# Two MLPs on one core: VectorE and ScalarE in a written order, weights three products ahead, own tiles for the second pair

## The chip, the cores and the metric

The kernel runs on one core of one Trainium2 chip. The metric is the device time of one execution in microseconds (us); the median of three runs of the kernel before is 1119.15 us (1118.34 to 1121.95).

A core has a matrix engine (TensorE, PE in the profile, with its weight loads as PEld), three engines for elementwise work (VectorE = DVE, ScalarE = ACT, GpSimd = POOL), and a SyncE (SP) that here only issues transfers. Each engine works through its own list of instructions in order and waits on semaphores for the others. Matmuls write to PSUM, which is eight banks of 128 x 512 float32; everything else lies in SBUF.

## The reference, cut to what matters

Two layers on x (512 tokens, 1024 features, float32). Layer 0 mixes with stick-breaking attention, layer 1 with a gated linear recurrence; the change touches neither. Both end in the same MLP:

```python
D_MODEL, SEQ, DEPTH, D_FF = 1024, 512, 2, 4096

def squared_relu_mlp(h, w1, w2):          # w1: 1024 x 4096, w2: 4096 x 1024
    u = jax.nn.relu(h @ w1)
    return (u * u) @ w2

def reference(x, ...):
    for layer in range(DEPTH):
        h = rms_norm(x, norm_mix[layer])
        x = x + (stick_breaking_attention(h, ...) if layer % 2 == 0 else rglru_block(h, ...))
        h = rms_norm(x, norm_mlp[layer])
        x = x + squared_relu_mlp(h, mlp_w1[layer], mlp_w2[layer])
    return rms_norm(x, norm_final)
```

## The kernel before, in words

**Operands in two parts.** Every matrix operand is split into a high part of type fp32r, copied by ScalarE (`wh`, `xgh`, `bh`, `sh`), and a low part, the rest, subtracted by VectorE (`wl`, `xgl`, `bl`, `sl`). Each product of two blocks is then three matmuls (high x high, high x low, low x high). So every weight block costs a ScalarE copy of 128 x 1024 (line 1002), a VectorE subtraction of the same size (line 1003), and a place in the pool `wpool`, which holds four pairs `wh`, `wl`.

**The MLP in quarters.** The 4096 hidden features are worked off in four quarters of 1024 (`q4`). A quarter has an up part (h @ w1 for its 1024 columns, in two pairs p of 512) and a down part (times its 1024 rows of w2, in two groups g of 512 rows, added into the output tiles `c`). Quarter 0's up part is eight plain slabs (`squared`, line 790 on); the up parts of quarters 1 to 3 (`up`, line 898 on) and all down parts (`down`, line 1057 on) use a scheme of seven block products, P1 to P7, in place of eight. For this, weight blocks are added into each other: b11 is used for P1, then b12 is added for P5, then b22 for P6, then b21 for P4; b12 becomes P7's operand when b22 is added. These additions are done by VectorE (line 1022) for P5 and P6, and for P7 and P4 by a transfer from DRAM that adds into the tile (line 1017, issued by POOL). An up part is 2 x 7 products of 24 matmuls with 256 columns; a down part is 2 x 7 products of 12 matmuls with 512 columns. So a quarter has 28 products.

**From up to down.** The four results of a pair lie in one tile `u` of four slots (two halves i each). Products that share a PSUM bank are taken apart by copies into `kept` (line 926) and one VectorE instruction each (line 939). Relu and square follow on ScalarE (lines 940 and 788). The down part of a group needs seven operand blocks of its pair: the slots 0 to 2 as they are (split by lines 825 and 826 into blocks 0 to 2) and four sums of slots (line 835) as blocks 3 to 6. Group 0's blocks lie in `bh`, `bl`, group 1's in `sh`, `sl`. P1 needs block 0, P2 block 1, P5 block 5, P6 block 3, P3 block 4, P7 block 6, P4 block 2. There is one buffer for `u`, so pair 1's `u` is written when pair 0's has been split.

**What sets the order.** PE keeps the order of the program text: the down part is P1 0, P5 0, P1 1, P2 0, P5 1, and so on (name and group). For ScalarE, VectorE, POOL and SP a scheduler chooses the order at build time from its own timeline, with hints in the text (`tc.high_priority()`, `tc.issue_after(...)`). A product's weights are prepared in the text right before its matmuls (in the last quarter two to three products ahead). SP loads the weight blocks into six `b` tiles and the b21 blocks into three `raw` tiles. After each product of group 1, two collects add its banks into `c` (line 1046 on VectorE; line 1049 on ScalarE for the first use in layer 0). In quarter 0's down part of each MLP, VectorE and ScalarE also form the sums of x that the later up parts need (`sums_of_x`, `halves_of_sums`, lines 853 to 891).

Of the kernel before, what the change touches and what calls it, by code (L numbers as in the profile page):

```python
# [17 lines left out]
P = 128  # L18
# [30 lines left out]
def hybrid_encoder(  # L49
# [678 lines left out]

    class Mlp:
# [51 lines left out]
        def u_tile(self, p):  # L781

            if p not in self.u:
                self.u[p] = self.mp.tile([P, 2, 4, HS], F32, tag="u", name="u", bufs=1)
            return self.u[p]

        def square(self, t):
            self.squares = A.activation(t, t, AF.Square)

        def squared(self, c):  # L790
# [11 lines left out]
            A.activation(t, ps.rearrange("p (h n) -> p h n", h=2), AF.Relu)  # L802
# [19 lines left out]
        def split(self, p, i, of, to):  # L822
            h, l = (t[:, i, to, :] for t in self.places(p))
            u = self.u[p][:, i, of, :]
            self.high = A.copy(h, u)  # L825
            self.ready = V.tensor_tensor(l, u, f(h), ALU.subtract)  # L826

        def sums(self, p, i):

            u = self.u[p]  # L830
            for out, x, y, op in (
                (2, 3, 2, ALU.subtract), (3, 0, 3, ALU.subtract), (0, 2, 0, ALU.subtract),
                (1, 0, 1, ALU.add),
            ):
                V.tensor_tensor(u[:, i, out, :], u[:, i, x, :], u[:, i, y, :], op)
# [17 lines left out]
        def sums_of_x(self, k):  # L853
# [3 lines left out]
            for c in (k, C // 2 + k):  # L857
                g = col(f"mlp{self.layer}")[:, c : c + 1]
                with tc.issue_after(self.high.ins):
                    A.activation(x[c], x[c], AF.Identity, scale=g)  # L860
            with tc.issue_after(self.ready.ins):
                V.tensor_tensor(v[:, hi], u[:, hi], v[:, hi], ALU.subtract)
            V.tensor_tensor(u[:, hi], u[:, lo], u[:, hi], ALU.subtract)
            V.tensor_tensor(u[:, lo], v[:, hi], u[:, lo], ALU.subtract)
            V.tensor_tensor(v[:, lo], u[:, lo], v[:, lo], ALU.add)
# [12 lines left out]
        def halves_of_sums(self, k):  # L878
# [6 lines left out]
            A.copy(self.s2(k), u[:, lo])  # L885
            V.tensor_tensor(low[:, lo], u[:, lo], f(self.s2(k)), ALU.subtract)
            A.copy(s3, u[:, hi])
            V.tensor_tensor(low[:, hi], u[:, hi], f(s3), ALU.subtract)
            low = self.low(C // 2 + k)
            A.copy(self.s41[:, k, :], v)  # L890
            V.tensor_tensor(low, v, f(self.s41[:, k, :]), ALU.subtract)

        def replace(self):

            for i, t in enumerate(self.s3):
                A.copy(xgh[:, 2 * i : 2 * i + 2, HS:], f(t).rearrange("p (k n) -> p k n", k=2))

        def up(self, q4, p, unit, far):

            u = self.u_tile(p)  # L900
            banks, kept = {}, {}
            for name in ("P1", "P5", "P6", "P3", "P7", "P2", "P4"):
                w = [t.rearrange("p j n -> p (j n)") for t in self.block(unit, name, far)]
                w = [t.rearrange("p (k n) -> p k n", n=2 * P) for t in w]
                block, _, _, to, *_ = self.PRODUCTS[name]
                new = to not in banks
                if new:
                    banks[to] = self.bank()
                ps = banks[to]
                for i in range(2):  # L910
                    for k in range(C // 2):
                        h, l = self.xa(block, k)
                        wh, wl = (t[:, k, i * P : (i + 1) * P] for t in w)
                        for n, (m, y) in enumerate(((wh, h), (wl, h), (wh, l))):
                            PE.matmul(  # L915
                                ps[:, i * HS : (i + 1) * HS], m, y,
                                start=new and i == k == n == 0,
                                stop=i == 1 and k == C // 2 - 1 and n == 2,
                                skip_group_check=not new,
                            )  # L920
                three = ps.rearrange("p (i n) -> p i n", i=2)
                if name in ("P1", "P5", "P6", "P7"):

                    tag = "sq" if name in ("P1", "P7") else "r"
                    t = work.tile([P, S], F32, tag=tag, name="kept")
                    A.copy(t, ps)
                    kept[name] = t.rearrange("p (i n) -> p i n", i=2)
                if name in ("P1", "P5", "P6"):
                    continue
                slot, x, y, op = {  # L930
                    "P3": (1, three, kept.get("P6"), ALU.subtract),
                    "P7": (2, kept.get("P5"), kept.get("P7"), ALU.subtract),
                    "P2": (0, kept.get("P1"), three, ALU.add),
                    "P4": (3, three, None, None),
                }[name]
                t = u[:, :, slot, :]
# [607 lines left out]
```

## Time and profile before

| | |
|---|---|
| median of 3 runs | 1119.15 us |
| profiled execution, its own time | 1119.22 us |
| its span (first to last instruction) | 1117.5 us |
| granted TensorE clock, mean | 0.978 |
| MLP of layer 0 | about 250 to 600 us of the span |
| MLP of layer 1 | about 757 us to the end |
| first product of a down part, layer 0 | 294.17, 376.74, 464.20, 550.66 us |
| first product of a down part, layer 1 | 801.74, 885.53, 974.09, 1062.67 us |
| first product of an up part, layer 0 | 335.03, 424.74, 511.20 us |
| first product of an up part, layer 1 | 845.17, 933.82, 1022.43 us |

The starts are read from the timeline of PE (first matmul of each product). Windows between such starts show how long a stretch of known products took, how long each engine was busy in it, and which clock TensorE was granted (1.00 is full speed). A stretch that takes longer than the same products elsewhere has waits or a low clock in it.

### The profile page before, as it was taken

How to read it: one execution, taken by the hardware profiler on the slowest of the kernel's cores; microseconds unless marked ns; L12 is line 12 of the kernel's file. 1: busy time of each engine (PE TensorE's matmuls, PEld its weight loads, DVE VectorE, ACT ScalarE, POOL GpSimd, SP SyncE). 2: the span in 40 equal slices, each digit the busy share in tenths (PEclk: the TensorE clock that was granted, in tenths of full speed). 3: DMA queues.
4: the chain of work that ended last, by engine and by line, in shares of the span. 5: the costliest groups of instructions: out<-in, count | busy, mean ns of one | idle time of the engine just before them, and what ended most of it. 6: DMA issues, size and time to landing. Idle time of an engine off the chain costs nothing.

```text
span 1117.5 us, 15833 instructions
## 1 busy us (share of the span) xinstructions
PE 1059.0 (95%) x5868; PEld 910.4 (81%) x5868; DVE 865.9 (77%) x1118; ACT 680.5 (61%) x1037; POOL 201.1 (18%) x242
## 2 busy tenths in 40 slices
PE   9999999999999989989989999999989989979987
PEld 7888898888779779869868777888879869958965
DVE  7778787756796977977888778854797876976886
ACT  6767676645676635735745587746574834743754
POOL 2444443400101000000002563000000000000012
PEclk9999999999999989999989999999999989989989
DMA  7746454446456655655732784242356655555533
GB/s 234 195 118 164 112 148 100 151 136 250 75 161 138 151 163 133 152 151 144 206 60 91 184 193 132 79 167 80 65 147 153 147 134 152 142 131 154 152 54 94
DMA packets 53693, 156.27 MB, mean 140 GB/s; under 512 B 8816, under 2 KB 9584, under 8 KB 53616
## 3 DMA queue, kind: packets, MB, share of 16 engines
q1 hardware_dynamic: 43536, 120.13, 33.8%
q0 software_dynamic: 9504, 34.61, 19.2%
q8 instruction: 46, 0.75, 0.3%
q10 hardware_dynamic: 576, 0.52, 0.1%
q14 instruction: 31, 0.25, 0.1%
HBM read 133.22 MB, written 4.19 MB: 123 GB/s over the span
## 4 chain that ended last, share of the span: by engine, by line
PE 63%; DVE 15%; ACT 10%; issue 7%; DMA 4%; POOL 1%; SPq 0%; ACTq 0%; POOLq 0%; DVEq 0%
PE ps_t L1035 8%; PE ps_acc L1035 6%; PE ps_z L915 6%; PE ps_acc L212 4%; PE ps_acc L210 4%; PE ps_acc L211 4%; PE ps_o L915 4%; DVE wl L1003 3%; PE ps_acc L915 3%; DMA b<-in_w_up 3%; ACT wh L1002 2%; DVE c L1046 2%; DVE sl L826 2%; PE ps_o L210 2%; PE ps_o L211 2%
## 5 line engine op out<-in xcount | busy, mean ns | idle before, releaser
L1002 ACT CAST wh<-b 128x1024 fp32r<-128x1024 f32 x168 | 174.0, 1047 | 176.9 <-DVE b L1022 79.4
L1003 DVE TENSOR_TENSOR wl<-b,wh 128x1024 fp32r<-128x1024 f32 x168 | 204.8, 1225 | 75.7 <-ACT wh L1002 75.5
L198 ACT CAST wh<-raw 128x512 fp32r<-128x512 f32 (+2 forms) x88 | 69.4, 818 | 47.1 <-DMA raw<-in_w_in 10.2
L1017 POOL DMA_DIRECT2D b<-in_w_dn x32 | 28.1, 877 | 364.9 <-DVE b L1022 238.9
L210 PE MATMUL ps_acc<-xgh,wh 128*128 128x512 f32 x208 | 85.0, 408 | 1.0 <-ACT wh L179 1.0
L205 DVE TENSOR_TENSOR wl<-raw,wh 128x512 fp32r<-128x512 f32 (+2 forms) x78 | 71.3, 941 | 18.3 <-ACT wh L198 18.1
L211 PE MATMUL ps_acc<-xgh,wl 128*128 128x512 f32 x208 | 81.6, 392 | 0.3 <-DVE wl L180 0.3
L212 PE MATMUL ps_acc<-xgl,wh 128*128 128x512 f32 x208 | 81.5, 392 | 0.1
L1017 POOL DMA_DIRECT2D b<-in_w_up x24 | 20.9, 871 | 305.6 <-DVE b L1022 198.4
L562 DVE TENSOR_TENSOR_SCAN scan<-keep,later 128x128 f32<-128x128 f32 (+1 forms) x64 | 58.0, 909 | 18.0 <-ACT keep L552 9.5
L1022 DVE TENSOR_TENSOR b<-b,b 128x1024 f32<-128x1024 f32 x56 | 68.3, 1219 | 0.4
L566 POOL TENSOR_TENSOR w<-w,scan 128x128 f32<-128x128 f32 (+1 forms) x64 | 51.9, 813 | 55.7 <-DVE scan L562 52.9
L1035 PE MATMUL ps_acc<-wh,sh 128*128 128x512 f32 x64 | 31.8, 496 | 26.5 <-ACT sh L825 18.2
L1035 PE MATMUL ps_t<-wh,sl 128*128 128x512 f32 x126 | 50.1, 397 | 5.7 <-DVE sl L826 5.7
L915 PE MATMUL ps_z<-xgh,wh 128*128 128x256 f32 x192 | 54.2, 282 | 0.0
L915 PE MATMUL ps_z<-xgh,wl 128*128 128x256 f32 x192 | 54.2, 282 | 0.0
L1035 PE MATMUL ps_t<-wh,sh 128*128 128x512 f32 x126 | 50.1, 398 | 4.0 <-ACT sh L825 4.0
L915 PE MATMUL ps_acc<-low,wh 128*128 128x256 f32 x192 | 53.7, 280 | 0.0
L1035 PE MATMUL ps_t<-wl,sh 128*128 128x512 f32 x126 | 49.8, 395 | 0.2 <-DVE wl L1003 0.2
L1035 PE MATMUL ps_t<-wh,bh 128*128 128x512 f32 x126 | 49.6, 394 | 0.0
L1035 PE MATMUL ps_t<-wl,bh 128*128 128x512 f32 x126 | 49.2, 391 | 0.0
L1035 PE MATMUL ps_t<-wh,bl 128*128 128x512 f32 x126 | 49.2, 390 | 0.0
(405 smaller groups left out, 3455.4 us busy)
## 6 DMA issues: line engine op xcount, KB each, us to landing
b<-in_w_dn SPq DMA_DIRECT2D x48, 512.0 KB, 5.9
b<-in_w_up SPq DMA_DIRECT2D x36, 512.0 KB, 3.5
b<-in_w_dn POOLq DMA_DIRECT2D x32, 512.0 KB, 5.5
b<-in_w_up POOLq DMA_DIRECT2D x24, 512.0 KB, 5.6
raw<-in_w_m SPq DMA_DIRECT2D x16, 512.0 KB, 3.9
raw<-in_w_dn SPq DMA_DIRECT2D x16, 512.0 KB, 4.5
raw<-in_w_in SPq DMA_DIRECT2D x16, 512.0 KB, 4.7
raw<-in_w_qk SPq DMA_DIRECT2D x12, 512.0 KB, 3.7
```

The source lines that it names most:

```text
L198: A.copy(wh[:, k, :], raw[:, k, :])
L205: V.tensor_tensor(wl[:, k, :], raw[:, k, :], f(wh[:, k, :]), ALU.subtract)
L210: PE.matmul(ps, wh, ah, start=start, stop=False)
L211: PE.matmul(ps, wl, ah, start=False, stop=False)
L212: PE.matmul(ps, wh, al, start=False, stop=stop)
L562: V.tensor_tensor_scan(sc[:, S - n : S][:, ::-1], keep[:, :n][:, ::-1], later[:, S - n :][:, ::-1], 1.0, ALU.mult, ALU.max,)
L566: G.tensor_tensor(wt, wt, sc[:, S - n + 1 : S + 1], ALU.mult)
L915: PE.matmul(ps[:, i * HS : (i + 1) * HS], m, y, start=new and i == k == n == 0, stop=i == 1 and k == C // 2 - 1 and n == 2, skip_group_che ...
L1002: A.copy(wh, raw)
L1003: self.cut = V.tensor_tensor(wl, raw, f(wh), ALU.subtract)
L1022: self.sum = V.tensor_tensor(raw, raw, unit[to], ALU.add)
L1035: PE.matmul(ps, m, y[:, jj, cols], start=first and n == 0, stop=last and n == 2, skip_group_check=not new,)
```

## The change

What it does:

- A wrapper `Ordered` around VectorE and ScalarE chains each instruction that the MLP issues through it behind the one before, so these two engines keep the order of the text. (In the profile all such instructions then carry one line, that of the wrapper.) The ScalarE collects of layer 0 and the plain slabs are not wrapped.
- One loop `run` over all products of the four quarters replaces `up`, `down` and the loop over quarters. Entering step i, `leave(i - 1)` first issues what follows the product that has just been queued on PE, and with it `prepare(i + 3)`: the weights of the product three further on. An up part's P7 weights are made together with P2's.
- Pair 1's four results lie in four work tiles (two `sq`, two `r`), which also take the copies that were in `kept`. Each slot is split into its operand block when its product is done (block 1 after P3, block 2 after P7, block 0 after P2); of the four sums block 5 is split first, blocks 3, 4 and 6 between the first down products (`waiting`). Pair 0's blocks 3 to 6 are split during pair 1's first products.
- The transfers that add for P7 and P4 are issued right after the weights of P5 and P6 have been cut. In every down part P6's addition for group 0 becomes such a transfer as well. That is eight more transfers of 512 KB in the program and eight fewer VectorE additions.
- Half of the sums of x (k = 0, 1) moves from quarter 0's down part into its slabs, and the squares of x stand with the first two slabs instead of the second to fifth. Quarter 0's down order becomes "mid" (P1 1 ahead of P2 0); the last one of layer 1 has P2 1 behind P5 1.

The diff, cut:

```diff
+    class Ordered:
+        def __getattr__(self, name):
+            def do(*args, **kwargs):
+                with tc.issue_after(self.prev.ins) if self.prev else nullcontext():
+                    ins = getattr(self.e, name)(*args, **kwargs)
+                if self.on:
+                    self.prev = ins
+                return ins
...
         def __init__(self, ctx, layer):
+            self.V, self.A = Ordered(V), Ordered(A)
...
-            self.high = A.copy(h, u)
-            self.ready = V.tensor_tensor(l, u, f(h), ALU.subtract)
+            self.A.copy(h, u)
+            self.ready = self.V.tensor_tensor(l, u, f(h), ALU.subtract)
...
+        def slots_of(self, p):
+            if p == 0:
+                u = self.u_tile(p)
+                return [u[:, :, j, :] for j in range(4)]
+            tags = ("sq", "sq", "r", "r")
+            return [
+                work.tile([P, S], F32, tag=t, name="u").rearrange("p (i n) -> p i n", i=2) for t in tags
+            ]
+        def split_slot(self, p, t, to):
+            h, l = (a[:, :, to, :] for a in self.places(p))
+            self.A.copy(h, t)
+            self.V.tensor_tensor(l, t, f(h), ALU.subtract)
...
         ORDERS = {
-            "first": "P1 0 P5 0 P2 0 P1 1 P5 1 P6 0 P6 1 P3 0 P3 1 P7 0 P7 1 P2 1 P4 0 P4 1",
             "mid": "P1 0 P5 0 P1 1 P2 0 P5 1 P6 0 P6 1 P3 0 P3 1 P7 0 P7 1 P2 1 P4 0 P4 1",
-            "last": "P1 0 P5 0 P2 0 P1 1 P2 1 P5 1 P6 0 P6 1 P3 0 P3 1 P7 0 P7 1 P4 0 P4 1",
+            "last": "P1 0 P5 0 P1 1 P2 0 P5 1 P2 1 P6 0 P6 1 P3 0 P3 1 P7 0 P7 1 P4 0 P4 1",
         }
+        UP = "P1", "P5", "P6", "P3", "P7", "P2", "P4"
...
+            FARS = [("P6", 0)]
+            def make(i):
...
+                name = steps[i][3]
+                ws[i] = made[i] = self.operand(self.source(unit(i), name))
+                for before, x in (("P5", "P7"), ("P6", "P4")):
+                    if name == before:
+                        self.added(unit(i), x)
+            def prepare(i):
+                if i < len(steps) and steps[i][0] == "up" and steps[i][3] == "P7":
+                    return
+                if i - 1 in range(len(steps)) and i - 1 not in made and i > 2:
+                    make(i - 1)
+                if i < len(steps) and steps[i][0] == "down":
+                    add(i, 0)
+                    if waiting and place(i) in (20, 22, 23):
+                        self.split_slot(*waiting.pop(0))
+                make(i)
+                for n in range(i + 1, i + 6):
+                    add(n, n - i)
...
+            def leave(i):
+                ahead = i + 4
...
+                if kind == "down":
+                    if p:
+                        for n in range(2):
+                            self.collect(name, n, bank[n])
+                    prepare(ahead)
...
+                if op:
+                    self.V.tensor_tensor(u[at], x, y, op)
+                if name == "P4":
+                    self.A.activation(u[3], three, AF.Relu)
+                    self.square(u[3])
+                    if p:
+                        last_sums(u, self.SUMS[:2])
...
+                prepare(ahead)
...
+                elif name == "P4" and p:
+                    last_sums(u, self.SUMS[2:3])
+                    self.split_slot(p, u[2], 5)
+                    last_sums(u, self.SUMS[3:])
+                    waiting[:] = [(p, u[j], 3 + j) for j in (0, 1, 3)]
...
+            for i, (kind, q4, g, name) in enumerate(steps):
+                load(i)
+                leave(i - 1)
```

How instructions move, at two places on VectorE. First, quarter 2 of layer 0 after pair 1's blocks 0 to 2: `u` is pair 1's results, `sl` the low parts of its blocks, `wl` a weight's low part, `b11<-b11,b12` an addition for P5, `b11<-b11,b22` one for P6, `c` a collect. Before:

```order
L1003 TENSOR_TENSOR wl_5154<-b11_4832,wh_5153 128x1024
L835 TENSOR_TENSOR u_4834<-u_4834 128x2x256
L1003 TENSOR_TENSOR wl_5173<-b11_4828,wh_5172 128x1024
L1046 SCALAR_TENSOR_TENSOR c0_3126<-ps_t_5081,rr_3442,c0_3126 128x512
L1022 TENSOR_TENSOR b11_4832<-b11_4832,b22_5075 128x1024
L835 TENSOR_TENSOR u_4834<-u_4834 128x2x256
L1046 SCALAR_TENSOR_TENSOR c0_3126<-ps_t_5082,rr_3442,c0_3126 128x512
L835 TENSOR_TENSOR u_4834<-u_4834 128x2x256
L1003 TENSOR_TENSOR wl_5190<-b11_4832,wh_5189 128x1024
L835 TENSOR_TENSOR u_4834<-u_4834 128x2x256
L1003 TENSOR_TENSOR wl_5208<-b22_5073,wh_5207 128x1024
L826 TENSOR_TENSOR sl_5029<-u_4834,sh_5028 128x1024 x2
```

The same place now, from the first of the four sums:

```order
L738 TENSOR_TENSOR u_4850<-u_4851,u_4850 128x512
L738 TENSOR_TENSOR u_4851<-u_4848,u_4851 128x512
L738 TENSOR_TENSOR wl_5091<-raw_5088,wh_5090 128x1024
L738 TENSOR_TENSOR u_4848<-u_4850,u_4848 128x512
L738 TENSOR_TENSOR sl_5012<-u_4850,sh_5011 128x2x256
L738 TENSOR_TENSOR u_4849<-u_4848,u_4849 128x512
L738 TENSOR_TENSOR wl_5113<-b11_4735,wh_5112 128x1024
L738 TENSOR_TENSOR wl_5132<-b11_4731,wh_5131 128x1024
L738 SCALAR_TENSOR_TENSOR c0_3126<-ps_t_5098,rr_3470,c0_3126 128x512
```

The four sums stood among four weights' low parts, two collects and an addition, and all of blocks 3 to 6 were split behind them; now one weight stands among the sums, and block 5 is split ahead of the last sum and of P5 1's weights (`wl_5113`).

Second, where pair 1's slots are written. Before, behind both splits of pair 0's blocks 3 to 6 (`bl`):

```order
L826 TENSOR_TENSOR bl_82<-u_4593,bh_81 128x1024
L1022 TENSOR_TENSOR b11_4828<-b11_4828,b12_4830 128x1024
L826 TENSOR_TENSOR bl_82<-u_4593,bh_81 128x1024
L1003 TENSOR_TENSOR wl_5097<-b11_4828,wh_5096 128x1024
L939 TENSOR_TENSOR u_4834<-ps_o_4871,kept_4927 128x2x256
L939 TENSOR_TENSOR u_4834<-kept_4896,kept_4989 128x2x256
L939 TENSOR_TENSOR u_4834<-kept_4864,ps_o_5000 128x2x256
```

Now, from the last split of pair 0:

```order
L738 TENSOR_TENSOR bl_82<-u_4615,bh_81 128x1024
L738 TENSOR_TENSOR u_4849<-ps_o_4878,u_4849 128x512
L738 TENSOR_TENSOR wl_4979<-b11_4731,wh_4978 128x1024
L738 TENSOR_TENSOR b11_4731<-b11_4731,b12_4733 128x1024
L738 TENSOR_TENSOR u_4850<-u_4850,u_4851 128x512
L738 TENSOR_TENSOR sl_5012<-u_4849,sh_5011 128x2x256
L738 TENSOR_TENSOR wl_5016<-b11_4731,wh_5015 128x1024
L738 TENSOR_TENSOR sl_5012<-u_4850,sh_5011 128x2x256
L738 TENSOR_TENSOR u_4848<-u_4848,ps_o_5025 128x512
L738 TENSOR_TENSOR wl_5052<-b11_4735,wh_5051 128x1024
L738 TENSOR_TENSOR b11_4735<-b11_4735,b12_4971 128x1024
L738 TENSOR_TENSOR sl_5012<-u_4848,sh_5011 128x2x256
```

The three instructions that write slots stood in one run; now each stands at its own product, with the split of its block close behind, and a weight for the coming down part at each.

More of the change, by code (lines that the diff above doesn't have):

```diff
@@ L889, in halves_of_sums @@
             low = self.low(C // 2 + k)
[L890 to L891 removed]
+            self.A.copy(self.s41[:, k, :], v)
+            self.V.tensor_tensor(low, v, f(self.s41[:, k, :]), ALU.subtract)
         def replace(self):
             for i, t in enumerate(self.s3):
[L896 to L936, printed above, removed]
[L937 to L947 removed]
@@ L1100, in hybrid_encoder, with order, part @@
-        FAR_UP, FAR_DOWN = ('P7', 'P4'), ('P7', 'P4')
-        def quarters(self, between, far, end):
-            for c in range(C):
+        def order(self, kind):
+            order = self.ORDERS[kind].split()
+            return [(name, int(g)) for name, g in zip(order[::2], order[1::2])]
+        def part(self, sums, name, g, w):
+            to = self.PRODUCTS[name][3]
+            if to not in sums:
+                sums[to] = [self.bank() for _ in range(2)]
+            for i in range(2):
+                self.times(name, g, i, w, sums[to][i], name in ("P1", "P5", "P2"))
@@ L1104, in quarters @@
+        def quarters(self, between, end):
+            for c in range(C - 1):
                 self.squared(c)
@@ L1192, in hybrid_encoder @@
         end.ready = back
-        mlp.quarters(between, ("P7", "P4"), end)
+        mlp.quarters(between, end)
         begin = [bank("acc") for _ in range(2)]
@@ L1473, in hybrid_encoder @@
         end.ready = factors
-        mlp.quarters(between, ("P7", "P4"), end)
+        mlp.quarters(between, end)
 COLS = {}
```

295 lines of the change are left out of this document (186 added, 109 removed).

## The prediction

> **What bounds the kernel now.** I read the page first, then PE's waits, then windows of equal work.
>
> ```profile
> PE 1059.0 (95%) x5868; PEld 910.4 (81%) x5868; DVE 865.9 (77%) x1118; ACT 680.5 (61%) x1037; POOL 201.1 (18%) x242
> PEclk9999999999999989999989999999999989989989
> PE ps_acc L1035 <- ACT sh L825: 18.2, 6, 4.1
> PE ps_acc L1035 <- ACT wh L1002: 8.3, 2, 4.4
> PE ps_t L1035 <- DVE sl L826: 5.7, 6, 1.1
> ...
> PE ps_z L915 <- ACT kept L926: 1.1, 2, 0.8
> ...
> PE ps_acc L915 <- ACT kept L926: 0.5, 1, 0.5
> ```
>
> PE is the bound, and what it loses it loses in few places: the longest waits (total us, times, longest) are all at line 1035, the down products, and most are for `sh`, `sl`, pair 1's operands. The clock dips at the same spots. Windows tell what these spots cost. Columns: length, then busy us (and count) of PE, PEld, DVE, ACT, POOL, granted clock, DMA share, GB/s. The first six run from the first product of each down part of quarters 1 to 3, in both layers, to the product behind P5 1: five products, six in the last.
>
> ```profile
> 376.74:400.00 23.26, 17.33 (x63) 12.61 (x62) 19.18 (x20) 12.12 (x15) 2.61 (x3) 0.86 0.63 126
> 464.20:486.58 22.38, 16.17 (x63) 11.79 (x62) 19.20 (x20) 12.02 (x15) 2.63 (x3) 0.92 0.65 131
> 550.66:574.18 23.52, 17.29 (x62) 12.76 (x61) 18.13 (x19) 12.12 (x15) 1.75 (x2) 0.86 0.41 80
> 885.53:908.86 23.33, 17.31 (x62) 12.62 (x61) 19.29 (x20) 12.12 (x15) 2.60 (x3) 0.85 0.63 125
> 974.09:997.35 23.26, 17.36 (x63) 12.61 (x61) 19.19 (x20) 12.13 (x15) 2.62 (x3) 0.86 0.61 125
> 1062.67:1087.09 24.42, 19.20 (x75) 14.65 (x73) 19.83 (x21) 12.97 (x16) 1.73 (x2) 0.86 0.25 38
> sum 140.17, PE 104.66 PEld 77.03 DVE 114.82 ACT 73.48 POOL 13.95; mean PE 17.44 PEld 12.84 DVE 19.14 ACT 12.25 POOL 2.32
> ...
> 486.58:511.20 24.62, 24.62 (x109) 20.27 (x108) 18.15 (x20) 8.39 (x8) 0.86 (x1) 1.00 0.49 139
> 511.20:550.66 39.46, 39.46 (x337) 39.46 (x336) 31.37 (x32) 28.00 (x35) 3.49 (x4) 1.00 0.71 198
> ```
>
> The last two rows are the undisturbed measure: nine down products in 24.62 us, so 2.74 each, and an up part of 14 products in 39.46. The six windows hold 31 products, 31 x 24.62/9 = 84.8 us at that pace. They took 140.17. **55.4 us** are lost there, some in waits, the rest at half clock behind them.
>
> Why PE waits there is in VectorE's and ScalarE's timeline of the second one (start, us, engine, line; in brackets idle time and its releaser). P4 of pair 1 ends at 464.2.
>
> ```profile
> 462.73 0.68 DVE L939 TENSOR_TENSOR u<-ps_o,kept 128x512 f32<-128x512 f32 x1
> ...
> 470.61 1.76 DVE L826 TENSOR_TENSOR sl<-u,sh 128x1536 fp32r<-128x1536 f32 x1 [1.46 <-ACT sh L825]
> 472.28 1.22 DVE L1003 TENSOR_TENSOR wl<-b,wh 128x1024 fp32r<-128x1024 f32 x1
> 473.42 0.68 DVE L835 TENSOR_TENSOR u<-u 128x512 f32<-128x512 f32 x1
> ...
> 479.94 0.69 DVE L835 TENSOR_TENSOR u<-u 128x512 f32<-128x512 f32 x1
> 480.55 1.22 DVE L1003 TENSOR_TENSOR wl<-b,wh 128x1024 fp32r<-128x1024 f32 x1
> 481.74 2.36 DVE L826 TENSOR_TENSOR sl<-u,sh 128x1024 fp32r<-128x1024 f32 x2
> 467.41 0.61 ACT L940 ACTIVATE u<-u 128x512 f32<-128x512 f32 x1
> 467.93 1.14 ACT L788 ACTIVATE u<-u 128x512 f32<-128x512 f32 x2
> 480.67 1.99 ACT L825 CAST sh<-u 128x1024 fp32r<-128x1024 f32 x2 [1.56 <-DVE u L835]
> ```
>
> Pair 1's first slot is written at 462.7, although its product P3 had ended long before; relu and square end at 469.0, blocks 0 to 2 follow at 470.6, and the four sums, 2.7 us of work, stretch from 473.4 to 480.6 because the scheduler put other work between them. P5 1, which needs only block 5, starts at 481.7.
>
> **The change, part by part.**
>
> ```profile
> 294.17:309.70 15.53, 14.22 (x61) 11.11 (x60) 12.45 (x23) 10.80 (x15) 2.62 (x3) 1.00 0.51 72
> 801.74:820.17 18.43, 15.62 (x62) 12.13 (x60) 16.42 (x25) 13.32 (x19) 2.60 (x3) 0.91 0.55 94
> 335.03:376.74 41.71, 40.41 (x337) 39.87 (x336) 32.27 (x32) 28.69 (x37) 4.31 (x5) 1.00 0.65 157
> 845.17:885.53 40.36, 40.15 (x337) 39.94 (x336) 32.41 (x33) 27.50 (x35) 3.48 (x4) 1.00 0.68 163
> 933.82:974.09 40.27, 40.15 (x337) 39.94 (x336) 31.28 (x32) 27.70 (x35) 3.49 (x4) 1.00 0.61 158
> 1022.43:1062.67 40.24, 40.15 (x337) 39.95 (x336) 31.27 (x32) 27.70 (x35) 3.49 (x4) 1.00 0.62 158
> 464.20:550.66 86.46, 80.25 (x506) 71.52 (x505) 68.72 (x71) 48.41 (x58) 6.99 (x8) 0.98 0.63 164
> 250.30:294.17 43.87, 43.87 (x199) 36.23 (x197) 32.40 (x45) 25.50 (x37) 1.03 (x1) 1.00 0.58 194
> ```
>
> *Own tiles and early splits (down starts of quarters 1 to 3).* Pair 1's slots no longer wait for pair 0's tile, so blocks 1, 2 and 0 are split behind P3, P7 and P2; only slot 3 and the sums are left when P4 ends. From then (E), with the durations above: relu 0.61 and square 0.57 to E+1.2; two sums of 0.68 to E+2.5; P2 0's low part, 1.14 from start to start, to E+3.7; the third sum to E+4.4; block 5's low part 0.7 to E+5.1 (ScalarE's copy lies beside the third sum); the last sum and P5 1's weights to E+6.9. P5 1 comes four products later, at E+10.9. VectorE isn't free at E: by the rows' durations it has 2.9, 2.9 and 3.5 us at P3, P7 and P2 of pair 1 against 2.8 of PE, and each split waits for relu, square and copy; I carry 2 us. So 2 us of margin, and blocks 3, 4, 6 have three products each. Cost not seen in the trace: what is left per start. Below, 0; above, one whole product, 2.74, or 16 us for six. I take 0.5 each, nearer the lower end because of the margin: 55.4 - 3 = **52.4 us** gone.
>
> *Starts of quarter 0.* Two windows, 33.96 us for ten products that need 27.4: 6.6 lost. Here the chain (split, four half sums, split) is only reordered, and P2 0's weights, cut into the buffer that the last slab frees, stand between. From the slab's end: relu and square 1.2, split to 3.0, P1 1's weights 4.2, sums 5.6, an addition and P2 0's weights 7.9, split 9.1, P5 1's weights 10.3, against 10.9. Tight: between 0 and 6.6, I leave 1 us each: **4.6 us** gone.
>
> *Up parts.* Against 39.46 the four rows lose 2.3, 0.9, 0.8 and 0.8, together 4.7; the few waits at line 915, the up products, are for copies of a bank (`kept`) by ScalarE. In the written order that copy comes first at each product, but behind older weight copies. Between 0 and 4.7 gained; I take **2.4**.
>
> *Wrapped order in itself.* It adds no instruction. VectorE's work per 28 products is 68.7 us (row 464.20:550.66); one addition goes (1.2), seven splits of 0.7 take the place of one of 1.76 and two of 1.2 (+0.7): 68. ScalarE 48.4 + 0.9. At PE's pace 28 products take 14 x 2.74 + 39.46 = 77.8 us, so VectorE may stand idle for 9.8 us of them and ScalarE for 28. That is the cover; without it each us of VectorE's idle time above 9.8 costs six (six such quarters).
>
> *Sums of x and squares moved.* They go into a stretch where VectorE has 43.87 - 32.40 = 11.5 us free and out of one where it was packed; the slabs' weights stand ahead of them. Cost 0; a slab late by all of one addition would cost 1.2.
>
> *Transfers.* The adding transfers for P7 and P4 start earlier, and P6 for group 0 joins them: nine on POOL in 28 products instead of eight, in the order P7 0, P6 0, P7 1, P4 0, P4 1 of a down part. SP's loads keep their sequence; only loads of x and of the final scales change places around the last three weight loads.
>
> ```profile
> DMA to landing us min/median/max: 5.3/5.6/8.5
> ACT wh L1002 <- DMA b<-in_w_up: 12.3, 6, 3.5
> ```
>
> P6 0's transfer can start when P5 0's low part is cut, about 7 us into the product after P3's end, and lands some 6.5 later; ScalarE reaches the copy about there, and PE needs it three products on. Cost 0, at most 8.5 - 5.6 = 2.9 a time, some 8 x 2.9 = 23 if nothing hid it.
>
> The sum is made against the profiled execution's 1119.22 us (span 1117.5), which is within 0.1 of the runs' median: 1119.2 - 52.4 - 4.6 - 2.4 = 1059.8, say **1060 us**.
>
> On the low clock: window 801.74:820.17 shows 0.91, and there no single wait was long.
>
> ```profile
> 814.94 0.50 PE L1035 MATMUL ps_acc<-wh,sh 128*128 128x512 f32 x1 [1.38 <-ACT sh L825]
> 817.11 0.80 PE L1035 MATMUL ps_acc<-wh,sl 128*128 128x512 f32 x1 [1.43 <-DVE sl L826]
> ```
>
> Two waits of 1.4 us cost 2.8 themselves and 4.75 in all, so the half clock took most of the other 1.9. [...] The sum stands by single waits; with the clock lost at both quarter-0 starts it would be 1063.6.
>
> **The rivals.**
>
> *Some waits move.* The order is fixed, so VectorE and ScalarE now stand behind whichever input is late. For it: VectorE waits 86.46 - 68.72 = 17.7 us in a quarter today, and 9.8 is what it may. Against it: much of this idle time is that of the down start itself. If 13.5 us stay, each quarter is 3.7 longer: 1060 + 6 x 3.7 = 1082 us. With all 17.7, 1060 + 47 = 1107, hardly better than now.
>
> *Slower: ScalarE blocked by the adding transfers.* `wh<-b` for P7, P4 and P6 0 waits for a landing; behind it on ScalarE stand the copies that free PE's banks and each relu. It has made ScalarE wait six times, up to 3.5 us. Nine such transfers lie in 28 products; if each delays PE by 1.5 us, a quarter gets 13.5 longer, against 59.4/6 = 9.9 saved: 1119 + 6 x 3.6 = 1141 us. It decides from 1.1 us each. Against it: the transfers are issued products earlier than before, so 6.5 us of landing have about 8 to hide in.
>
> *Nothing comes of it.* If the waits came from ScalarE's total work and not from order, they would stay at about 1115. But ScalarE is busy for 12.1 of 23.3 us in these windows.
>
> **How the numbers follow.** My forecast, 1060 (1052 to 1070): 0.72. Waits move, 1070 to 1107: 0.19. Nothing, 1107 to 1123: 0.03. Slower, from 1123: 0.06. The low end is every loss gone: 1119.2 - 55.4 - 6.6 - 4.7 = 1052.5, and 0.5 for the rest. The upper end takes a whole product at each down start, 1060 + 13, and some of the first rival: 1083. Some 2 in 10 lie outside. The kernel's measurement tells 0.3% (3.4 us) from no change. Faster takes the first two and half the third, 0.92; same 0.02; slower 0.06.
>
> **What would show it.** Right: the six down starts take 13.7 to 15 us for five products at clock 1.00; `sh`, `sl` all but vanish from PE's waits; slots of pair 1 are written within a product of their matmuls; PE's busy share rises to 98%. Wrong: windows of 28 products well over 80 us with PE waiting for `wh` or `wl` in the middle of a part; ScalarE's waits for `b<-in_w_up` and `b<-in_w_dn` above the 12.3 us of now; a clock under 1.00 inside an MLP.

## The result, and the profile after

The changed kernel takes 1056.87 us (median of 4 runs, 1054.7 to 1058.39) against 1119.2 us of the kernel before: a ratio of 0.9438, 95% interval 0.9414 to 0.9461. The forecast was 1060, range 1052 to 1083. The profiled execution took 1057.16 us, its span is 1055.5.

The page of the changed kernel, engines and granted clock:

```profile
PE 1039.0 (98%) x5868; PEld 904.5 (86%) x5868; DVE 858.1 (81%) x1134; ACT 686.9 (65%) x1061; POOL 208.4 (20%) x250
PEclk9999999999999999999999999999999999999999
```

Its waits of PE and of ScalarE, those that belong to the MLPs (total us, times, longest):

```profile
PE ps_z L947 <- ACT u L738: 0.8, 1, 0.8
ACT wh L738 <- DMA b<-in_w_up: 1.9, 1, 1.9
ACT wh L738 <- DMA b<-in_w_dn: 1.5, 1, 1.5
```

PE's waits for `sh`, `sl`, `wh` in the down products are gone from the list; one wait of 0.8 us is left in both MLPs together. The same windows as before the change, first product of a down part to the product behind P5 1 (line 1042 is now the down matmul, 947 the up matmul, 738 every ordered instruction of VectorE and ScalarE). The last down part of layer 1 is again counted over six products, so that its row holds the same work as before:

```profile
...
450.61:464.29 13.68, 13.68 (x62) 11.27 (x61) 12.81 (x17) 8.57 (x12) 2.60 (x3) 1.00 0.73 150
...
851.58:865.39 13.81, 13.81 (x63) 11.28 (x61) 12.94 (x17) 8.57 (x13) 2.62 (x3) 1.00 0.74 148
...
1009.04:1025.66 16.62, 16.62 (x75) 13.54 (x74) 15.04 (x18) 9.99 (x14) 2.62 (x3) 1.00 0.51 92
sum 85.28, PE 85.28 PEld 69.92 DVE 79.52 ACT 52.41 POOL 15.67; mean PE 14.21 PEld 11.65 DVE 13.25 ACT 8.74 POOL 2.61
...
294.66:308.61 13.95, 13.95 (x61) 11.19 (x60) 11.79 (x21) 9.24 (x12) 1.74 (x2) 1.00 0.34 75
771.57:785.58 14.01, 14.01 (x62) 11.19 (x61) 11.65 (x15) 7.02 (x8) 1.73 (x2) 1.00 0.32 73
...
411.15:450.61 39.46, 39.46 (x337) 39.45 (x336) 31.79 (x32) 28.77 (x38) 3.49 (x4) 1.00 0.62 155
810.57:851.58 41.01, 40.23 (x338) 40.01 (x336) 34.81 (x37) 30.11 (x40) 3.46 (x4) 1.00 0.60 153
...
450.61:528.55 77.94, 77.94 (x506) 70.93 (x505) 67.62 (x74) 49.20 (x62) 7.85 (x9) 1.00 0.71 184
```

| stretch | before | after | difference |
|---|---|---|---|
| six down starts, quarters 1 to 3 | 140.17 | 85.28 | -54.9 |
| two starts of quarter 0 | 33.96 | 27.96 | -6.0 |
| six up parts | 241.5 | 239.2 | -2.3 |
| everything else (rest of the span's -62.0) | | | +1.2 |

In the six windows PE is busy for the whole length at full clock. But VectorE's timeline of quarter 2, layer 0, shows how close that is. P4 of pair 1 ends at 450.61, P5 1 starts at 461.54:

```profile
445.26 0.68 DVE L738 TENSOR_TENSOR u<-ps_o,u 128x512 f32<-128x512 f32 x1
...
448.25 0.68 DVE L738 TENSOR_TENSOR u<-u 128x512 f32<-128x512 f32 x1
...
451.30 0.69 DVE L738 TENSOR_TENSOR sl<-u,sh 128x512 fp32r<-128x512 f32 x1 [0.62 <-ACT sh L738]
451.90 0.68 DVE L738 TENSOR_TENSOR u<-u,ps_o 128x512 f32<-128x512 f32 x1
452.50 1.22 DVE L738 TENSOR_TENSOR wl<-b,wh 128x1024 fp32r<-128x1024 f32 x1
453.75 1.22 DVE L738 TENSOR_TENSOR b<-b,b 128x1024 f32<-128x1024 f32 x1
454.90 0.68 DVE L738 TENSOR_TENSOR sl<-u,sh 128x512 fp32r<-128x512 f32 x1
...
458.84 0.69 DVE L738 TENSOR_TENSOR sl<-u,sh 128x512 fp32r<-128x512 f32 x1
...
460.05 2.35 DVE L738 TENSOR_TENSOR wl<-b,wh 128x1024 fp32r<-128x1024 f32 x2
```

P2's slot (`u<-u,ps_o`) is written at 451.90, behind P4's end, and block 0 is cut at 454.90. Block 5 is ready at 459.5 and P5 1's weights, the first of the two in the last row, at about 461.2, a third of a microsecond ahead of P5 1.

### The profile page after: what moved, and what is told of

Its sections match the earlier page's. It is cut to its first block, busy times and chain, and to the rows that moved or that the text cites. A ratio compares the mean times of both kernels' runs of the same rounds, so it can differ in the third digit from the quotient of the medians.

```text
span 1055.5 us, 15891 instructions
## 1 busy us (share of the span) xinstructions
PE 1039.0 (98%) x5868; PEld 904.5 (86%) x5868; DVE 858.1 (81%) x1134; ACT 686.9 (65%) x1061; POOL 208.4 (20%) x250
## 4 chain that ended last, share of the span: by engine, by line
PE 82%; DVE 7%; ACT 4%; DMA 3%; issue 2%; SPq 0%; POOL 0%; ACTq 0%; DVEq 0%; POOLq 0%
PE ps_t L1042 14%; PE ps_acc L947 8%; PE ps_z L947 8%; PE ps_acc L1042 7%; PE ps_o L947 5%; PE ps_acc L211 4%; PE ps_acc L212 4%; PE ps_acc L210 4%; PE ps_z L1042 4%; PE ps_t L211 2%; PE ps_t L210 2%; PE ps_t L212 2%; PE ps_o L210 2%; PE ps_o L211 2%; PE ps_o L212 2%
## 5 line engine op out<-in xcount | busy, mean ns | idle before, releaser
L1024 POOL DMA_DIRECT2D b<-in_w_dn x40 | 35.0, 875 | 363.8 <-DVE b L738 269.4
L198 ACT CAST wh<-raw 128x512 fp32r<-128x512 f32 (+2 forms) x88 | 69.3, 817 | 41.9 <-DMA raw<-in_w_in 10.9
L562 DVE TENSOR_TENSOR_SCAN scan<-keep,later 128x128 f32<-128x128 f32 (+1 forms) x64 | 58.5, 915 | 18.3 <-ACT keep L552 13.4
L738 ACT ACTIVATE u<-u 128x512 f32<-128x512 f32 x100 | 63.1, 632 | 6.5 <-DVE u L738 4.8
L738 DVE TENSOR_TENSOR b<-b,b 128x1024 f32<-128x1024 f32 x48 | 58.7, 1223 | 1.3
L738 DVE TENSOR_TENSOR u<-u 128x512 f32<-128x512 f32 (+1 forms) x92 | 54.8, 596 | 2.7 <-ACT u L738 1.1
```

What stands on the lines that cost most here:

```text
L198: A.copy(wh[:, k, :], raw[:, k, :])
L562: V.tensor_tensor_scan(sc[:, S - n : S][:, ::-1], keep[:, :n][:, ::-1], later[:, S - n :][:, ::-1], 1.0, ALU.mult, ALU.max,)
L738: ins = getattr(self.e, name)(*args, **kwargs)
L1024: G.dma_start(out=unit[b].rearrange("p j n -> p (j n)"), in_=unit["src"](to), accum_op=ALU.add)
```

## The experiments

The total came out as forecast; the question was whether for the reasons given. Three things changed at the six starts: pair 1 got tiles of its own and is split early and piece by piece (theory A: that is what counts), VectorE and ScalarE keep a written order (theory B), and weights are made three products ahead (theory C). The table holds what the windows gave, each read from that kernel's own product starts; the sum of the six windows or the row that a reading rests on is shown below. The down parts behind the starts and the rest of the kernel are not columns; where they move, the text says so.

| kernel | time, us | six starts | quarter 0 | up parts |
|---|---|---|---|---|
| before | 1119.2 | 140.2 | 34.0 | 241.5 |
| changed | 1056.9 | 85.3 | 28.0 | 239.2 |
| order written, one tile | 1054.75 | 85.3 | 28.0 | 239.1 |
| order free, own tiles | 1073.0 | 86.3 | 40.7 | 238.3 |
| order free, one tile | 1115.25 | 132.8 | 41.0 | 238.4 |
| before + own tiles and pieces | 1080.5 | 95.3 | 34.1 | 242.4 |
| before + pieces | 1093.4 | 112.0 | 34.1 | 241.7 |
| blocks 0 to 2 late | 1061.5 | 89.5 | 28.0 | 239.2 |
| one tile, coarse pieces | 1071.3 | 98.3 | 28.0 | 239.6 |
| order on VectorE alone | 1093.65 | 111.9 | 30.4 | 252.6 |
| weights two ahead | 1082.6 | 104.5 | 28.0 | 249.1 |
| P6 0 added by VectorE | 1072.1 | 91.5 | 29.1 | 239.6 |
| 1.8 us more on VectorE | 1066.9 | 95.7 | 28.0 | 239.4 |
| 4.8 us more on VectorE | 1097.5 | 129.2 | 28.0 | 239.5 |

### Own tiles or written order

One tile for pair 1, order written:

```diff
-            tags = ("sq", "sq", "r", "r")
-            return [work.tile([P, S], F32, tag=t, name="u")... for t in tags]
+            self.u[p] = u = self.mp.tile([P, 2, 4, HS], F32, tag="u", name="u", bufs=1)
+            return [u[:, :, j, :] for j in range(4)]
...
-                    self.A.copy(u[keep], three)
+                    kept[name] = work.tile([P, S], F32, tag=tag, name="kept")...
+                    self.A.copy(kept[name], three)
```

> The changed kernel, but pair 1's results go into the one tile u again, copies of banks into separate kept tiles; the written order is the same row for row. Theory A as my prediction put it (own tiles): the write of pair 1's first slot waits until pair 0's last blocks are cut, each start loses several us, 1085 us or more. Theory B: no change, 1055 to 1060 us, since VectorE cuts pair 0's last block at 444.12 to 445.3 us in the trace of the change and writes the first slot of pair 1 at 445.26, so the tile is free by the written order itself.

Measured 1054.75 us (1054.01 to 1055.91), ratio to before 0.9423 (0.9403 to 0.9443). The six windows:

```profile
sum 85.27, PE 85.27 PEld 69.91 DVE 79.35 ACT 53.26 POOL 15.66; mean PE 14.21 PEld 11.65 DVE 13.22 ACT 8.88 POOL 2.61
```

The own tiles bring nothing once the order is written: theory B's case. (The 2 us against the changed kernel lie outside these windows, and the intervals overlap.)

The order left to the scheduler, own tiles kept:

```diff
-            for e in (self.V, self.A):
-                e.turn(True)
```

> The changed kernel with nothing chained: text, tiles, splits and weights three products ahead as in the change, but the scheduler chooses VectorE's and ScalarE's order in the MLPs. Theory A: most of the gain stays, 1060 to 1075 us. Theory B: the four sums and the splits drift behind weights and collects again, 1090 to 1119 us, with PE waiting for sh and sl at the down products.

Measured 1072.99 us. Its six windows, and the two of quarter 0:

```profile
sum 86.27, PE 85.69 PEld 69.76 DVE 83.43 ACT 59.26 POOL 15.66; mean PE 14.28 PEld 11.63 DVE 13.90 ACT 9.88 POOL 2.61
...
294.44:312.92 18.48, 15.64 (x61) 12.16 (x60) 17.33 (x39) 10.75 (x13) 1.76 (x3) 0.89 0.67 138
781.78:804.02 22.24, 16.24 (x62) 12.16 (x61) 18.88 (x30) 9.85 (x13) 2.60 (x3) 0.85 0.54 118
```

Theory A's number, and a sharper picture than it had: at the six starts the written order is worth 1 us, at quarter 0's two starts, where pair 1 has no tiles of its own in either kernel, 12.8 us. Another 5.7 us lie in what follows the starts in the six earlier down parts (155.0 us here, 149.3 in the changed kernel).

Both taken away:

```diff
-            for e in (self.V, self.A):
-                e.turn(True)
...
+            self.u[p] = u = self.mp.tile([P, 2, 4, HS], F32, tag="u", name="u", bufs=1)
```

> The changed kernel with nothing chained and one tile u with kept copies: against the unchained one with own tiles (1073 us) only the tiles differ. Theory A2: the same, 1070 to 1077 us. Theory B2 (without a written order the tiles are needed): 1090 us and above, the loss at the six down starts of quarters 1 to 3.

Measured 1115.25 us, nearly the kernel before. VectorE's timeline of quarter 2, layer 0 (P4 of pair 1 ends at 462.68), and the sum of the six windows:

```profile
458.81 1.22 DVE L738 TENSOR_TENSOR bl<-u,bh 128x1024 fp32r<-128x1024 f32 x1
...
461.21 0.68 DVE L738 TENSOR_TENSOR u<-ps_o,kept 128x512 f32<-128x512 f32 x1
461.81 0.68 DVE L738 TENSOR_TENSOR u<-kept 128x512 f32<-128x512 f32 x1
462.41 0.68 DVE L738 TENSOR_TENSOR u<-kept,ps_o 128x512 f32<-128x512 f32 x1
```

```profile
sum 132.81, PE 101.55 PEld 78.01 DVE 111.53 ACT 77.43 POOL 16.02; mean PE 16.93 PEld 13.00 DVE 18.59 ACT 12.90 POOL 2.67
```

The scheduler puts pair 0's last split behind an addition, and with one tile all three slots of pair 1 must follow it in a run, at 461.2 to 463.1. So at the six starts either of the two is enough, and without both 47.5 us return (132.81 - 85.28). The written order splits pair 0 early and needs no tile. How the tiles help where no order is written is less clear. With own tiles and no order the first slot of pair 1 is written at 451.36, ahead of pair 0's last two splits, but the other two come behind them as well (456.50 and 457.10, with P4's end at 457.50). The first sum then starts 6.6 us after P4's end, here 10.4. The scheduler made another order of all of VectorE's work around the one tile, and no run separates the tile's wait from that order.

### The same parts on the kernel before

Pair 1 in four tiles and in pieces, scheduler's order, weights right ahead of their product; then pieces alone, in one tile:

```diff
+                own = kept[{1: "P6", 2: "P5", 0: "P1", 3: "P7"}[slot]]
+                t = own if p else u[:, :, slot, :]
...
+                    if p and name != "P4":
+                        self.split_slot(p, t, slot)
...
+                    for n, (out, x, y, op) in enumerate(self.SUMS):
+                        V.tensor_tensor(own[out], own[x], own[y], op)
+                        if n == 2:
+                            self.split_slot(p, own[2], 5)
+                    for j in (0, 1, 3):
+                        self.split_slot(p, own[j], 3 + j)
```

> The kernel before, with pair 1's part of the change alone: its four results lie in the four tiles that held the copies of the banks, each is split into its block behind its own square, block 5 behind the third sum. The scheduler still chooses every engine's order, weights are made right ahead of their product. Theory A (own tiles and early splits carry the gain): the six down starts of quarters 1 to 3 lose most of their 55.4 us, 1065 to 1080 us. Theory B (the written order carries it): the scheduler still spreads the four sums among weights and additions, 1100 to 1119 us.

> The kernel before with pair 1 cut in pieces alone: one tile u as before, but each slot split behind its own square, block 5 behind the third sum, blocks 3, 4 and 6 one by one behind the last; the scheduler chooses the order. Theory A2 (size of the pieces: before, one instruction per half held all of blocks 3 to 6 behind the last sum): about the 1080 us that pieces and own tiles together took. Theory B2 (the tile: the scheduler writes pair 1's three slots in one run behind pair 0's last split): 1100 to 1119 us.

Measured 1080.51 us, just above theory A's range, and 1093.37 us. The sums of the six windows, first of the one with own tiles, then of the one without:

```profile
sum 95.25, PE 90.40 PEld 71.67 DVE 91.15 ACT 57.64 POOL 10.43; mean PE 15.07 PEld 11.94 DVE 15.19 ACT 9.61 POOL 1.74
```

```profile
sum 111.97, PE 95.46 PEld 73.47 DVE 106.17 ACT 74.50 POOL 12.09; mean PE 15.91 PEld 12.25 DVE 17.70 ACT 12.42 POOL 2.01
```

Without any order and any lead, own tiles and pieces take 44.9 of the 54.9 us at the six starts, of which pieces alone take 28.2. Neither range of the second expectation held: both effects are there. The kernel with own tiles gives 7.2 us back behind the starts (156.9 us in the six earlier down parts, 149.7 before). And with pieces, one tile and no written order the starts take 112.0 us here, but 132.8 with the rest of the change around them: what one tile costs depends on the order that the scheduler finds.

### The size and the place of the pieces

Blocks 0 to 2 split behind P4, ahead of the sums, order written:

```diff
-                            self.split_slot(p, u[at], at)
...
+                    for at in (0, 1, 2):
+                        self.split_slot(p, u[at], at)
+                    last_sums(u, self.SUMS[:3])
```

> The changed kernel, order still written, but pair 1's blocks 0 to 2 are all split behind P4, ahead of the sums. Theory A (early splits are most of the 52.4 us): each of the six starts loses 4 us or more, 1080 us and above. Theory B: only three instructions of 0.6 us move behind P4's end; against a margin of about 0.3 us (P5 1's weights were ready at 461.3, it started at 461.54) that is 1.5 us for each start, 9 us in all and some clock, 1062 to 1075 us.

Measured 1061.5 us (1058.98 to 1062.58), just under theory B's range. The six windows:

```profile
sum 89.54, PE 88.22 PEld 68.96 DVE 81.81 ACT 53.23 POOL 15.67; mean PE 14.70 PEld 11.49 DVE 13.64 ACT 8.87 POOL 2.61
```

The starts lose 89.54 - 85.28 = 4.3 us, 0.7 each. Early splits are worth 4 us here, not the bulk of 52.4.

Coarse pieces as before the change, one tile (its lines as above), order written:

```diff
...
-                    self.split_slot(p, u[2], 5)
-                    last_sums(u, self.SUMS[3:])
-                    waiting[:] = [(p, u[j], 3 + j) for j in (0, 1, 3)]
+                    for n in range(2):
+                        self.split(p, n, slice(0, 4), slice(3, 7))
```

> The changed kernel with one tile u, kept copies and pair 1 cut as coarsely as before (blocks 0 to 2 in one instruction behind P2's square, the four sums in a row, blocks 3 to 6 in two instructions of half a pair each); the order of VectorE and ScalarE stays written, weights three ahead. Theory E (the order or the tiles, either is enough; the pieces are worth only VectorE's added work): from P7's slot on VectorE has about 13.3 us in place of 11.75 up to P5 1's weights, so each of six starts loses 1.6 to 2.5 us, 1063 to 1071 us. Rival (the size of the pieces is most of the 55 us): 1080 us and above.

Measured 1071.3 us. The six windows:

```profile
sum 98.27, PE 88.78 PEld 68.92 DVE 92.79 ACT 59.94 POOL 15.70; mean PE 14.80 PEld 11.49 DVE 15.46 ACT 9.99 POOL 2.62
```

That is 13.0 us at six starts, 2.2 each, as theory E's count of VectorE's work gave; the total is 0.3 above its range. So under a written order and three products of lead, everything the change does to pair 1's data is worth some 14 us (1071.3 against 1056.9). The kernel is still 48 us faster than the one before; what it keeps of the change is the order, the lead, pair 0's early splits, the earlier transfers with that for P6 0, the order of the down products and the places of the x sums.

### Half an order

```diff
-            for e in (self.V, self.A):
-                e.turn(True)
+            self.V.turn(True)
```

> The changed kernel with VectorE's order written and ScalarE's left to the scheduler. Without any written order only quarter 0's two starts lost (40.7 us against 28.0). Theory F (there VectorE's order is what matters, since the four half sums and collects are its work): 1055 to 1062 us. Rival G (ScalarE's: copies of weights ahead of sh): about 1068 to 1073 us, the two starts near 40 us.

Measured 1093.65 us: both ranges missed, and 21 us more than with no order at all. Quarter 0's starts come back to 30.4 us, so theory F was right about them, but the six starts take 111.9 us and the up parts 13.4 us more than in the changed kernel. VectorE and ScalarE in quarter 2, layer 0:

```profile
462.88 0.69 DVE L738 TENSOR_TENSOR sl<-u,sh 128x512 fp32r<-128x512 f32 x1 [3.23 <-ACT sh L738]
```

```profile
457.34 2.00 ACT L738 CAST wh<-b 128x1024 fp32r<-128x1024 f32 x2 [0.44 <-DVE b L738]
459.24 1.04 ACT L738 CAST wh<-raw 128x1024 fp32r<-128x1024 f32 x1
...
462.24 0.61 ACT L738 CAST sh<-u 128x512 fp32r<-128x512 f32 x1
```

The scheduler lets ScalarE copy three weights ahead of relu, square and `sh`, and VectorE, held to its order, stands for 3.23 us with all its later work behind it. ScalarE's order alone was not run.

### How much room VectorE has

Three more instructions of 0.6 us behind the last sum, each taking the larger of a slot and itself:

```diff
                     last_sums(u, self.SUMS[3:])
+                    last_sums(u, ((1, 1, 1, ALU.max),) * 3)
```

> The changed kernel with three more VectorE instructions of 0.6 us, 1.8 us in all, behind the last sum of pair 1 in quarters 1 to 3 (each takes the larger of a slot and itself, so values stay). My prediction's margin of 2 us at P5 1: no change, 1055 to 1059 us. The margin read from the changed kernel's trace, about 0.3 to 0.5 us (P5 1's weights end at 461.3, it starts at 461.54 and reads the low part 0.23 later): 1.3 to 1.5 us lost at each of six starts, 8 to 9 us and perhaps some clock, 1064 to 1072 us.

Measured 1066.88 us, as the margin from the trace gave. Windows and PE's timeline of quarter 2, layer 0:

```profile
452.12:467.64 15.52, 13.97 (x63) 11.20 (x61) 14.55 (x20) 8.46 (x12) 2.60 (x3) 1.00 0.62 131
...
sum 95.70, PE 86.97 PEld 69.40 DVE 89.97 ACT 51.67 POOL 15.70; mean PE 14.49 PEld 11.57 DVE 15.00 ACT 8.61 POOL 2.62
```

```profile
465.00 0.50 PE L1042 MATMUL ps_acc<-wl,sh 128*128 128x512 f32 x1 [1.54 <-DVE wl L738]
```

Of 1.8 us added, (95.70 - 85.28)/6 = 1.74 were lost at each start. The margin was not 2 us but about nothing, less even than the 0.3 to 0.5 read from the trace.

P6's addition for group 0 back on VectorE:

```diff
-            FARS = [("P6", 0)]
+            FARS = []
```

> The changed kernel with P6's addition for group 0 on VectorE in every down part, as before the change, in place of the adding transfer: 1.2 us more VectorE work behind P5 1's weights and eight transfers fewer. My prediction took the transfer's cost as nothing and the margin of VectorE as 2 us: 1055 to 1059 us. With the margin of next to nothing that the padded run showed, P6 0's low part comes some 0.3 to 1.2 us late in eight down parts: 1059 to 1067 us. Rival (the adding transfers hold ScalarE up): under 1054 us.

Measured 1072.09 us, above every range. VectorE and PE in quarter 2, layer 0:

```profile
466.13 1.23 DVE L738 TENSOR_TENSOR wl<-b,wh 128x1024 fp32r<-128x1024 f32 x1 [1.17 <-ACT wh L738]
467.27 1.40 DVE L738 SCALAR_TENSOR_TENSOR c<-ps_t,rr,c 128x512 f32<-128x512 f32 x2
```

```profile
468.16 0.47 PE L1042 MATMUL ps_t<-wh,bh 128*128 128x512 f32 x1 [1.14 <-DVE c L738]
472.26 0.50 PE L1042 MATMUL ps_t<-wl,sh 128*128 128x512 f32 x1 [0.76 <-DVE wl L738]
```

One addition of 1.2 us costs twice: it makes ScalarE copy P6 0's weights late, VectorE waits 1.17 us for that copy, and behind it stand the two collects that PE needs for a free bank. Then P6 1's weights are late too. The text puts the addition right ahead of that copy; whether it would cost less in another place was not run. Starts and quarter 0 lose 6.2 and 1.2 us, and the rest of the six earlier down parts 6.9 (149.3 us in the changed kernel, 156.1 here).

Weights two products ahead:

```diff
-                ahead = i + 4
+                ahead = i + 3
```

> The changed kernel with weights prepared two products ahead in place of three, order still written. Theory C (three ahead is needed): P2 0's weights now stand behind the last sum, ready at about 9.4 us after P4's end, and P2 0 is due at 8.2, so each of six starts loses 1.2 us and some clock; VectorE's waits in the middle of parts come on top: 1065 to 1080 us. Theory D (any lead that covers a copy and a subtraction, 2.3 us, does): 1055 to 1060 us.

Measured 1082.6 us, a little above theory C's range. PE in quarter 2, layer 0, and the sum of the six windows:

```profile
465.13 0.50 PE L1042 MATMUL ps_t<-wl,sh 128*128 128x512 f32 x1 [1.15 <-DVE wl L738]
469.33 0.50 PE L1042 MATMUL ps_z<-wl,bh 128*128 128x512 f32 x1 [1.16 <-DVE wl L738]
```

```profile
sum 104.53, PE 90.43 PEld 68.98 DVE 94.92 ACT 58.33 POOL 20.94; mean PE 15.07 PEld 11.50 DVE 15.82 ACT 9.72 POOL 3.49
```

19.2 us go at the starts and 9.9 in the up parts (249.1 against 239.2): the rest of the kernel is 3.9 us shorter. With the order fixed, the third product of lead is worth 26 us.

Eight more instructions, to see what a long wait costs:

```diff
+                    last_sums(u, ((1, 1, 1, ALU.max),) * 8)
```

> The changed kernel with eight more VectorE instructions of 0.6 us, 4.8 us, behind the last sum of pair 1 in quarters 1 to 3; three of them cost 1.74 us a start and no clock. If a long wait costs only itself: 1057 + 6 x 4.7 = 1085 us at clock 0.99 and more. If a wait over 4 us halves the clock behind it for 3.4 us, as in the kernel before: 1.7 us more each, 1095 us and above, clock 0.98 or under.

Measured 1097.47 us at clock 0.982, the second case. The window and PE in quarter 2, layer 0:

```profile
457.12:478.49 21.37, 16.19 (x62) 12.82 (x61) 19.66 (x27) 9.70 (x14) 2.60 (x3) 0.85 0.56 107
```

```profile
473.63 0.80 PE L1042 MATMUL ps_acc<-wl,sh 128*128 128x512 f32 x1 [5.18 <-DVE wl L738]
```

The start lost 21.37 - 13.68 = 7.7 us: 5.2 of waiting, 2.5 of half clock behind it; over the six it is 7.3 on average (129.2 against 85.3). This wait cost more than itself. So did one of 4.04 us in the same quarter of the kernel before, which ended at 481.76: the clock in the 4.82 us behind it was 0.65.

```profile
481.76:486.58 4.82, 4.50 (x13) 3.12 (x14) 3.10 (x4) 0.90 (x1) 0.00 (x0) 0.65 0.89 218
```

## Why the prediction was right, and where its steps were wrong

**The six down starts.** Forecast -52.4, measured -54.9: nothing is left, not 0.5 us a start. The cause as the prediction put it is not the one at work in this kernel: "Pair 1's slots no longer wait for pair 0's tile, so blocks 1, 2 and 0 are split behind P3, P7 and P2". Without the own tiles the written order is as fast (1054.75), with blocks 0 to 2 split behind P4 only 4.6 us slower. The gain has no single carrier. With the pieces and the lead in place, either own tiles or the order is enough, though the prediction gave the order no gain of its own here; under no order and one tile the starts take 132.8 us.

**The chain behind P4.** This step failed: "only slot 3 and the sums are left when P4 ends", block 5 at E+5.1, P5 1's weights at E+6.9, "2 us of margin". The term that was too small is the 2 us carried for VectorE's older work. With it the chain came to E+7.1 and E+8.9. Measured: block 5 at 459.5, E+8.9, the weights at about E+10.6, due at E+10.9. So the carried work is about 3.7 us, and of 2 us of margin about 0.3 is left. I had put each slot within a product, 2.8 us, behind its matmuls, and named that as a sign of being right; they are written 3.2 us (P3, ended 442.05), 3.4 (P7, 444.87) and 4.2 (P2, 447.73) after it, since VectorE's list has other work ahead of them (ahead of P3's slot a weight and pair 0's last split). So P2's slot, a weight, an addition and two splits of VectorE's stood behind E as well. That nothing was lost was a matter of 0.1 to 0.3 us, as 1.8 us of padding showed by costing 1.74. Here the right number was luck.

**Starts of quarter 0, up parts.** -6.0 against -4.6 and -2.3 against -2.4. For the first the written order is needed: with nothing chained they take 40.7 us, more than before the change. What the moved sums of x and P1 1 ahead of P2 0 do for these starts was not run apart. Of the up parts one loses: layer 1's first, 41.01 against 39.89 in the next two, with the one wait left, 0.8 us.

**Wrapped order in itself, weights ahead.** No cost, as said, and VectorE is idle for 77.94 - 67.62 = 10.3 us of 28 products where 9.8 were allowed for. But the lead of three products had no term of its own, and it is worth 26 us.

**Transfers.** That they cost nothing was right: ScalarE's waits for landings in the MLPs are 1.9 and 1.5 us, against 12.3 on `in_w_up` alone before. What the transfer for P6 0 saves was mis-sized: "one addition goes (1.2)" stood among VectorE's cover at no price, and without it the kernel is 15 us slower, since VectorE has no room at just that place.

**The rivals.** Waits did not move in the change itself, ScalarE was not blocked, and the case that nothing comes of it is out. The first rival's mechanism, VectorE standing behind an input that is late, is what the kernels with half an order (3.23 us at one wait) and with P6 0 on VectorE showed.

**The half clock.** No wait is left in the down parts, so the doubt at quarter 0 (1063.6) did not come up. The sum counts no clock for what it leaves at each start, 0.5 and 1 us; no run shows that for such losses. What the runs showed is the kernel padded with 1.8 us: six waits of up to 1.6 us at its starts, and the clock at 1.00 in its six windows. Of two like pairs of waits close together in one run, one lost clock and the other did not, as the last section shows.

So the sum was right and its reserve was not. The half us left to each start stood on a margin that hardly existed; what saved it was that every part of the change, lead, transfer and order, was in place.

## What to carry to other kernels

When several edits each give a late operand another way to be early, price them jointly: taken away one at a time here each looks worth 0 (tiles), 5 (early splits), 15 (P6's transfer), 16 (the order) or 26 us (the lead), and together 62. Be wary of fixing the order of one engine of a chain and not of its neighbour: here VectorE, held to its order, stood still behind whatever the free ScalarE put first, 3.23 us at one wait. And time such a chain through everything that stands ahead of it in each engine's list, as a trace shows it, not from the end of the matmuls.

## What the runs showed of the hardware

How much idle time brings the half clock was not settled. A single wait of 1.54 us left it at 1.00 (1.8 us of padding, window 452.12:467.64). In the kernel with half an order, quarters 1 and 3 of layer 0 have the same pair of waits, 2.2 us and 0.3 close behind. Quarter 1, then quarter 3:

```profile
382.11 0.51 PE L1042 MATMUL ps_t<-wh,sh 128*128 128x512 f32 x1 [2.24 <-ACT sh L738]
383.13 0.80 PE L1042 MATMUL ps_t<-wh,sl 128*128 128x512 f32 x1 [0.28 <-DVE sl L738]
```

```profile
550.45 0.50 PE L1042 MATMUL ps_t<-wh,sh 128*128 128x512 f32 x1 [2.23 <-ACT sh L738]
551.47 0.50 PE L1042 MATMUL ps_t<-wh,sl 128*128 128x512 f32 x1 [0.29 <-DVE sl L738]
```

The windows of these two down starts:

```profile
374.24:392.44 18.20, 15.68 (x63) 12.17 (x61) 14.90 (x19) 10.96 (x18) 2.87 (x4) 0.91 0.63 120
542.59:559.50 16.91, 14.39 (x62) 11.03 (x61) 13.61 (x18) 10.76 (x17) 2.86 (x4) 1.00 0.69 148
```

PE is idle for 2.52 us in each (18.20 - 15.68 and 16.91 - 14.39), but the first ran at 0.91 and the second at 1.00. So in this run the amount of idle time alone did not decide; what did was not shown.

One thing stays open: the same five products take 13.81 us in layer 1 and 13.68 in layer 0, with PE busy throughout at clock 1.00 (rows 851.58:865.39 and 450.61:464.29 of the windows after). No run looked into it.
